# Decode delta rule of a hybrid decoder step: new values spread by transposes, or by a broadcast read of DRAM

## The chip, the cores and the metric

The kernel runs on one core of one Trainium2 chip. The metric is the device time of one execution in microseconds. The profile is of one further execution; its times count from the start of its span.

## The reference, cut to what matters

One layer of a decoder, for 256 prompt tokens and 8 decode tokens (one for each of 8 batch entries): a normed input times a wide matrix `w_in`, sparse attention on one side, a gated delta rule on the other, gates, and three output projections. The change lies in the delta rule of the decode tokens. For each of 8 entries and 8 heads there is a state S of 128x128, and one step is

```python
S = exp(g) * S
v_new = beta * (v - k @ S)
S = S + outer(k, v_new)
o = q @ S
```

The kernel gets k @ S and q @ S from the old state (both scaled by exp(g)) and adds (k . q) v_new to the second, so that o is known before S is updated. The updated S is an output, 1 MB for each pair of entries.

## The kernel before, in words

Nearly all work is projections in fp32 by three products of fp32r parts. Weights come in halves of 128 x 8 x 128 (512 KB, `raw`, issued on SP, three buffers); ScalarE copies the high part `hi` (L332), VectorE subtracts the low part `lo` (L333; three buffers each), and TensorE does 24 matmuls `acc` per half (L205), into one of two PSUM buffers. Two halves make a unit of 128 output columns; the units of the first output projection (letters `p` and `P`) are of one half. A unit ends with its evacuation: to a gate (`ev_gate`, L1504), an output gate (`ev_z`, L1489 to L1493), or, for `p`, a VectorE operation that folds PSUM into the gate tile (L1511). The order of the units is the string `ORDER`.

Everything else is written as generators that run between the matmuls: the main loop (L1627 to L1636) loads half i+4, splits half i+2, multiplies half i in two parts, and after each part calls `tick()`, which lets each active generator go on to its next `yield` (`yield n` rests n ticks). So the place of an instruction in the program is set by ticks. The framework's planner then orders each engine's queue when the kernel is built: VectorE, ScalarE and TensorE as its own timing suggests, an instruction emitted later moving ahead of one that it takes for not ready. SP and POOL keep the emitted order (L165). On the chip every queue is in order.

`g_gdn_dec` (L1364) is the delta rule of the decode tokens, `g_gdn` (L1128) that of the prompt; both start after the last `qkv` unit and run side by side. `g_gdn_dec` goes through the 8 entries in four pairs (`b0`, L1429). For a pair it multiplies the state `sst` by k and q (`sw`, 16 matmuls), brings the rows back (`swr`, `swt`), and gets the new values `dvn` (L1445), 16 columns of 128, and the output `dod` (L1446, L1447). Then the update: a new value lies along the partitions, and must be the same in all partitions and run along the columns. So TensorE transposes one column, broadcast to 128x128, into PSUM, 64 times in all, four to a group (`vnb`):

```python
for hh in range(4):
    c = (4 * hg + hh) * 8 + b0 + b
    tr(p4[:, 128 * hh:128 * hh + 128], vn[:, c:c + 1].to_broadcast([128, 128]))
yield 3
```

ScalarE scales the state (L1459) and VectorE adds PSUM times k (L1460). After the pair ScalarE's queue stores the state (`o_Ss`, L1463) and loads that of the next pair but one. A pair takes 36 ticks by its yields. When all are done, `odec` lets `g_gdn` put the decode output into `oB`, which the `Z` units need (L1485 waits for it by ticking).

Large tiles share one pool of `NS` slots of 8448 bytes per partition (`slot`, L169). A tile takes a slot when one is free and gives it back after its last use. `g_gdn` uses POOL's queue for the triangular inverse: `At` goes to DRAM and back (`ad`, `prod`, L1190 and L1197), its result too (`td`, `U`, `TI`, L1210 to L1216). The conv state of the decode tokens, `cd`, has a tile of its own.

Of the kernel before, what the change touches and what calls it, by code (L numbers as in the profile page):

```python
# [144 lines left out]
def program(tc, A):  # L145
# [8 lines left out]

    NS = 13
    cp = pool("cp")
# [12 lines left out]
    def slot(name, shape, dt=F32):  # L169
        return s8.tile(shape, dt, tag="s8", name=name)  # L170
# [70 lines left out]
    acc2 = cp.tile([128, 128], F32, name="acc2")  # L241
    cd = cp.tile([128, 24, 3, NB], F32, name="cd")
    cpo = cp.tile([128, 24, 3], F32, name="cpo")
# [5 lines left out]
    S.activation(warm, warm, AF.Exp)  # L249

    active, rest = [], {}

# [248 lines left out]
    def g_qstat(h):  # L501
# [7 lines left out]
        if h == 7:  # L509
# [16 lines left out]
            for g in range(2):  # L526
                V.scalar_tensor_tensor(o[:, g], qr[:, 4 * g:4 * g + 4, :], P("qw"),
                                       rd.rearrange("p (g r b) -> p g r b", g=2, r=4)[:, g], ALU.mult, ALU.mult)
            qx = slot("qm", [128, 640])
            G.memset(qx, 0.0)  # L530
            L["qdp"] = qdp = qx[:, 0:128]
# [520 lines left out]
    def ev_qkv(j):  # L1052
        def f(ps):
            k, h = j // 8, j % 8
            if h == 0:
                L["qkv", k] = slot("qkvr", [128, 8, TT])
                if k == 0:
                    SP.dma_start(cd, A["cst8"])
                if k == 1:
                    L["ktk"] = slot("ktk", [128, 2, 8, 128])  # L1060
                if k == 2:
                    L["vbt"] = slot("vbt", [128, 2, 8, 128])
            r = L["qkv", k]
            S.activation(r[:, h, :], ps[:, 0:TT], AF.Copy)
            V.tensor_copy(cpo[:, j, :], r[:, h, TP - 3:TP])
            if j == 23:
                G.dma_start(A["o_conv"], cpo)
            if h == 7:
                G.dma_start(A["o_convs"][:, 8 * k:8 * k + 8, 2, :], r[:, :, TP:TT])
            start(g_conv(j))  # L1070
        return f
# [292 lines left out]
    def g_gdn_dec():  # L1364
# [7 lines left out]
        state(0)  # L1372
        state(2)
        G.dma_start(A["o_convs"][:, :, 0:2, :], cd[:, :, 1:3, :])
        cw = P("cw").rearrange("p (j i) -> p j i", i=4)
# [11 lines left out]
        V.scalar_tensor_tensor(cv, th, 1.0, cv, ALU.add, ALU.mult)  # L1387
        sq = tp.tile([128, 16, NB], F32, name="dsq", tag="dsq", bufs=2)
        S.activation(sq, cv[:, 0:16], AF.Square)
        x = tp.tile([72, 2, 64], F32, name="dx", tag="dsq", bufs=2)  # L1390
        V.memset(x, 0.0)
# [10 lines left out]
        mm(pt[:, 128:256], ones[0:72, :], x.rearrange("p a c -> p (a c)"))  # L1402
        r = tp.tile([128, 128], F32, name="dr", tag="dsq", bufs=2)
        rsq(r, pt[:, 0:128], 1.0, 4 * EPS, [128, 128])
        eb = tp.tile([128, 2, 64], F32, name="deb", tag="deb")
        S.activation(eb, pt[:, 128:256].rearrange("p (a c) -> p a c", a=2), AF.Copy)
# [4 lines left out]
        q, k, v = f64(cv[:, 0:8]), f64(cv[:, 8:16]), f64(cv[:, 16:24])  # L1411
        wq = tp.tile([128, 80, 2], F32, name="wq", tag="wq")
        V.memset(wq[:, 64:80], 0.0)
# [10 lines left out]
        V.tensor_copy(kq, p2[:, 0:64])  # L1424
        od = tp.tile([128, 64], F32, name="dod", tag="dod")
        vn = tp.tile([128, 64], F32, name="dvn", tag="dvn")
        hb3 = lambda a: a.rearrange("p (h b) -> p h b", h=8)
        yield 2
        for b0 in range(0, NB, 2):  # L1429
# [14 lines left out]
            a3 = lambda t: t.rearrange("p (h b) -> p b h", h=8)[:, b0:b0 + 2]  # L1444
            V.tensor_sub(a3(vn), a3(u), pv[:, 0])  # L1445
            V.tensor_mul(a3(od), a3(vn), a3(kq))  # L1446
            V.tensor_add(a3(od), a3(od), pv[:, 1])  # L1447
            yield 4
            for b in range(2):
                for hg in range(2):  # L1450
                    p4 = PGD("vnb")
                    for hh in range(4):
                        c = (4 * hg + hh) * 8 + b0 + b
                        tr(p4[:, 128 * hh:128 * hh + 128], vn[:, c:c + 1].to_broadcast([128, 128]))
                    yield 3
                    for hh in range(4):
                        h = 4 * hg + hh
                        c = h * 8 + b0 + b
                        S.activation(ss[:, b, h, :], ss[:, b, h, :], AF.Copy, scale=eb[:, 0, c:c + 1])  # L1459
                        V.scalar_tensor_tensor(ss[:, b, h, :], p4[:, 128 * hh:128 * hh + 128], k[:, c:c + 1],  # L1460
                                               ss[:, b, h, :], ALU.mult, ALU.add)
                    yield 4
# [239 lines left out]
def build(m):  # L1702
    nc = _bacc.Bacc("TRN2", target_bir_lowering=False, num_devices=1, dynamic_dma_scratch_size=8192)
    A = {}
    for k, a in m.items():
        A[k] = nc.dram_tensor(k, a.shape, mybir.dt.from_np(a.dtype), kind="ExternalInput").ap()
    for k, s in OUTS.items():
        A[k] = nc.dram_tensor(k, s, F32, kind="ExternalOutput").ap()
    with tile.TileContext(nc, schedule_with_timeline_sim=True) as tc:
        program(tc, A)  # L1710
    nc.finalize()
    return nc
# [29 lines left out]
```

## Time and profile before

| | |
|---|---|
| median of 3 runs | 1135.54 us (1135.36 to 1137.25) |
| the profiled execution | 1137.88 us |
| its span | 1136.2 us |
| granted TensorE clock, mean | 0.994 |
| TensorE (PE) busy | 1112.4 us, 98% |
| VectorE (DVE) busy | 697.1 us, 61% |
| ScalarE (ACT) busy | 572.7 us, 50% |
| POOL busy | 144.2 us, 13% |

Busy time is the time in which an engine has an instruction at work; matmuls overlap, so the start-to-start distance says what one costs. A group of instructions is written as line, engine, operation, output<-inputs. "Idle before" or square brackets name the wait just before an instruction and what ended it.

### The profile page before, as it was taken

What the parts mean: (1) busy time and instruction counts of PE and PEld (TensorE: products, weight loads), DVE (VectorE), ACT (ScalarE), POOL (GpSimd) and SP (SyncE); (2) the same over time, 40 slices, a digit from 0 to 9 for tenths busy, and PEclk for the clock granted to TensorE, in tenths of its full rate; (3) what the DMA queues carried; (4) which work ended last, traced back from release to release, by engine and by line L of the source; (5) the groups of instructions that cost most, each with busy time, mean ns of one, the idle gap of its engine ahead of it and who ended that gap; (6) DMA issues with size and microseconds to landing.
All of it is one profiled execution on the core that took longest, in us unless ns stands there. A gap on an engine that the chain in (4) does not pass through costs nothing.

```text
span 1136.2 us, 25323 instructions
## 1 busy us (share of the span) xinstructions
PE 1112.4 (98%) x9558; PEld 1069.3 (94%) x9558; DVE 697.1 (61%) x1523; ACT 572.7 (50%) x1138; POOL 144.2 (13%) x227
## 2 busy tenths in 40 slices
PE   4999999999999999999999999999999999999998
PEld 3989999999999987897989999999999999999998
DVE  3578565443657776783566577677547575487443
ACT  4445655444634766673454465545344554444332
POOL 4430244200001310113022100102000000000000
PEclk9989999999999999999999899999999999999999
DMA  9873676435445784568998755657454355556663
GB/s 302 255 241 124 202 205 203 152 95 160 161 138 177 218 214 135 159 196 220 281 390 291 268 174 176 201 179 220 138 187 148 119 165 177 181 184 223 201 236 125
DMA packets 77069, 222.17 MB, mean 196 GB/s; under 512 B 10625, under 2 KB 27850, under 8 KB 75410
## 3 DMA queue, kind: packets, MB, share of 16 engines
q1 hardware_dynamic: 59346, 164.36, 44.7%
q0 software_dynamic: 15008, 44.98, 13.8%
q10 hardware_dynamic: 2592, 11.21, 2.6%
q8 instruction: 75, 1.23, 0.4%
q14 instruction: 48, 0.39, 0.1%
HBM read 202.90 MB, written 17.60 MB: 194 GB/s over the span
## 4 chain that ended last, share of the span: by engine, by line
PE 92%; DVE 1%; ACT 0%; issue 0%; ACTq 0%
PE acc L205 77%; PE inv L205 1%; PE po L205 1%; PE gtr L202 1%; PE pvo L205 1%; PE ps L205 1%; PE gsc L205 1%; PE cf L205 1%; PE kk L205 1%; PE vnb L202 1%; PE uw L205 1%; DVE xt L306 1%; PE pst L202 0%; PE og L205 0%; PE wsc L205 0%; PE kvtr L202 0%
## 5 line engine op out<-in xcount | busy, mean ns | idle before, releaser
L333 DVE TENSOR_TENSOR lo<-raw,hi 128x1024 fp32r<-128x1024 f32 (+1 forms) x250 | 304.8, 1220 | 212.5 <-ACT hi L332 206.1
L205 PE MATMUL acc<-xh,hi 128*128 128x264 f32 (+1 forms) x1488 | 433.8, 292 | 0.0
L332 ACT ACTIVATE hi<-raw 128x1024 fp32r<-128x1024 f32 (+1 forms) x250 | 263.9, 1056 | 329.7 <-PE acc L205 269.0
L205 PE MATMUL acc<-xl,hi 128*128 128x264 f32 (+1 forms) x1488 | 426.9, 287 | 0.5 <-issue 0.5
L205 PE MATMUL acc<-xh,lo 128*128 128x264 f32 (+1 forms) x1488 | 426.3, 287 | 0.0
L205 PEld LDWEIGHTS acc<-xh,hi 128*128 128x128 f32 (+1 forms) x1488 | 281.0, 189 | 7.6 <-issue 7.0
L205 PEld LDWEIGHTS acc<-xh,lo 128*128 128x128 f32 (+1 forms) x1488 | 280.0, 188 | 2.7 <-issue 2.2
L205 PEld LDWEIGHTS acc<-xl,hi 128*128 128x128 f32 (+1 forms) x1488 | 281.1, 189 | 1.5 <-issue 1.0
L205 PE MATMUL acc<-hi,w1h 128*128 128x254 f32 (+1 forms) x512 | 148.1, 290 | 15.9 <-ACT hi L409 15.9
L205 PE MATMUL acc<-lo,w1h 128*128 128x254 f32 (+1 forms) x512 | 147.4, 288 | 3.4 <-DVE lo L410 3.2
L205 PE MATMUL acc<-hi,w1l 128*128 128x254 f32 (+1 forms) x512 | 145.7, 285 | 0.0
L410 DVE TENSOR_TENSOR lo<-rawc,hi 128x512 fp32r<-128x512 f32 (+2 forms) x136 | 84.0, 656 | 52.5 <-ACT hi L409 48.1
L205 PEld LDWEIGHTS acc<-hi,w1h 128*128 128x128 f32 x512 | 98.4, 192 | 16.0 <-ACT hi L409 15.9
L409 ACT ACTIVATE hi<-rawc 128x512 fp32r<-128x512 f32 (+2 forms) x136 | 74.7, 599 | 62.7 <-PE acc L205 58.0
L205 PEld LDWEIGHTS acc<-lo,w1h 128*128 128x128 f32 x512 | 99.2, 194 | 4.8 <-DVE lo L410 4.5
L205 PEld LDWEIGHTS acc<-hi,w1l 128*128 128x128 f32 x512 | 99.0, 193 | 0.1
L386 POOL DMA_DIRECT2D rawc<-ccmp x125 | 67.3, 538 | 98.2 <-issue 72.3
L205 PE MATMUL acc<-oh,hi 128*128 128x264 f32 x256 | 73.5, 287 | 0.0
L205 PE MATMUL acc<-oh,lo 128*128 128x264 f32 x256 | 72.9, 285 | 0.0
L205 PE MATMUL acc<-ol,hi 128*128 128x264 f32 x256 | 72.7, 284 | 0.0
L205 PE MATMUL acc<-mh,hi 128*128 128x264 f32 x256 | 72.6, 284 | 0.0
L205 PE MATMUL acc<-ml,hi 128*128 128x264 f32 x256 | 72.5, 283 | 0.0
(452 smaller groups left out, 1476.4 us busy)
## 6 DMA issues: line engine op xcount, KB each, us to landing
raw<-win SPq DMA_DIRECT2D x184, 512.0 KB, 3.5
raw<-wpab SPq DMA_DIRECT2D x32, 512.0 KB, 3.9
raw<-wo SPq DMA_DIRECT2D x32, 512.0 KB, 4.3
rawc<-ccmp SPq DMA_DIRECT2D x126, 128.0 KB, 2.7
rawc<-ccmp POOLq DMA_DIRECT2D x125, 128.0 KB, 3.3
raw<-w SPq DMA_DIRECT2D x8, 512.0 KB, 7.6
wk<-winK SPq DMA_DIRECT2D x8, 512.0 KB, 11.1
o_wk<-wk POOLq DMA_DIRECT2D x8, 512.0 KB, 9.0
```

What stands on the lines that cost most here:

```text
L202: T.transpose(out, in_, ident[0:n, 0:n])
L205: T.matmul(out, lhsT, rhs, start=start, stop=stop, **k)
L306: V.scalar_tensor_tensor(xt[i][:, k, :], xt[i][:, k, :], P("nw")[:, kk:kk + 1], rx, ALU.mult, ALU.mult)
L332: S.activation(self.hi, self.raw, AF.Copy)
L333: V.tensor_sub(self.lo, self.raw, self.hi)
L386: e.dma_start(rawc[kv, b][j // 8][:, j % 8].rearrange("p s c g -> p (s c g)"), src[kv, bass.ds(r, 1)].rearrange("o d f -> (o d) f"))
L409: S.activation(h, src, AF.Copy)
L410: V.tensor_sub(l, src, h)
```

## The change

The group transposes go. Per pair, one transpose brings the 16 columns of the new values into 16 rows (`p4[0:16]`), VectorE copies them to SBUF (`vr`), POOL's queue writes them to DRAM (`vd`, 8 KB), and then reads them back broadcast to all 128 partitions into a slot `vw` (1 MB). The new values lie pair by pair in `vnp`, 16 columns side by side, for that. After 7 ticks come the 64 updates, which read `vw` in place of PSUM. `keep_in_program_order` (`late`) ties each of these to the VectorE instruction emitted before it, so that the planner can't move it ahead. A pair takes 29 ticks. `NS` is 14. Room for the slot comes from the conv state, which now lies in the slot of `qm`, from small tiles of the decode delta rule, which now lie in the two buffers `zz` of attention, and from half the scratch for POOL's DMA descriptors.

```diff
-    NS = 13
+    NS = 14
...
-    cd = cp.tile([128, 24, 3, NB], F32, name="cd")
...
+    late = tc.keep_in_program_order
...
-            qx = slot("qm", [128, 640])
-            G.memset(qx, 0.0)
+            qx = slot("qm", [128, 1216])
+            G.memset(qx[:, 0:640], 0.0)
+            L["cd"] = qx[:, 640:1216].rearrange("p (j i b) -> p j i b", j=24, i=3)
...
+        za, zb = (tp.tile([128, 384], F32, name=n, tag="zz", bufs=2) for n in ("dga", "dgb"))
+        cd = L.pop("cd")
...
-        sq = tp.tile([128, 16, NB], F32, name="dsq", tag="dsq", bufs=2)
+        sq = zb[:, 0:128].rearrange("p (h b) -> p h b", b=NB)
...
-        od = tp.tile([128, 64], F32, name="dod", tag="dod")
-        vn = tp.tile([128, 64], F32, name="dvn", tag="dvn")
+        od, vn = za[:, 288:352], zb[:, 256:320]
+        vd = dp.tile([4, 16, 128], F32, name="vd")
...
-            V.tensor_sub(a3(vn), a3(u), pv[:, 0])
-            V.tensor_mul(a3(od), a3(vn), a3(kq))
+            vnp = vn[:, 8 * b0:8 * b0 + 16]
+            vn3 = vnp.rearrange("p (b h) -> p b h", b=2)
+            V.tensor_sub(vn3, a3(u), pv[:, 0])
+            V.tensor_mul(a3(od), vn3, a3(kq))
             V.tensor_add(a3(od), a3(od), pv[:, 1])
-            yield 4
+            yield 2
+            p4 = PGD("vnt")
+            tr(p4[0:16, 0:128], vnp)
+            vr = tp.tile([16, 128], F32, name="vnr", tag="a", bufs=NA)
+            V.tensor_copy(vr, p4[0:16, 0:128])
+            vw = slot("vw", [128, 2, 8, 128])
+            G.dma_start(vd[b0 // 2], vr)
+            G.dma_start(vw.rearrange("p b h d -> p (b h d)"),
+                        vd[b0 // 2:b0 // 2 + 1].rearrange("o r d -> o (r d)").to_broadcast([128, 2048]))
+            yield 7
             for b in range(2):
                 for hg in range(2):
-                    p4 = PGD("vnb")
-                    for hh in range(4):
-                        c = (4 * hg + hh) * 8 + b0 + b
-                        tr(p4[:, 128 * hh:128 * hh + 128], vn[:, c:c + 1].to_broadcast([128, 128]))
-                    yield 3
                     for hh in range(4):
                         h = 4 * hg + hh
                         c = h * 8 + b0 + b
                         S.activation(ss[:, b, h, :], ss[:, b, h, :], AF.Copy, scale=eb[:, 0, c:c + 1])
-                        V.scalar_tensor_tensor(ss[:, b, h, :], p4[:, 128 * hh:128 * hh + 128], k[:, c:c + 1],
-                                               ss[:, b, h, :], ALU.mult, ALU.add)
+                        late(V.scalar_tensor_tensor(ss[:, b, h, :], vw[:, b, h, :], k[:, c:c + 1], ss[:, b, h, :],
+                                                    ALU.mult, ALU.add))
                     yield 4
...
-    nc = _bacc.Bacc("TRN2", target_bir_lowering=False, num_devices=1, dynamic_dma_scratch_size=8192)
+    nc = _bacc.Bacc("TRN2", target_bir_lowering=False, num_devices=1, dynamic_dma_scratch_size=4096)
```

## Rows read from the trace of the kernel before

**Rows 1.** The page's busy times, share of the span, instructions.

```profile
PE 1112.4 (98%) x9558; PEld 1069.3 (94%) x9558; DVE 697.1 (61%) x1523; ACT 572.7 (50%) x1138; POOL 144.2 (13%) x227
```

**Rows 2.** TensorE's waits, 100 us to the end: total, times, longest.

```profile
PE pvo L205 <- ACT wP L798: 0.6, 1, 0.6
PE acc L205 <- issue: 0.5, 1, 0.5
```

**Rows 3.** The chain that ended last, shares of the span by line.

```profile
by line: PE acc L205 76.6%; PE inv L205 1.4%; PE po L205 1.4%; PE gtr L202 1.2%; PE pvo L205 1.2%; PE ps L205 1.0%; PE gsc L205 0.9%; PE cf L205 0.7%; PE kk L205 0.6%; PE vnb L202 0.6%; PE uw L205 0.6%; DVE xt L306 0.5%; PE pst L202 0.5%; P
```

**Rows 4.** Windows: stretch, length, busy (x instructions) PE, PEld, DVE, ACT, POOL; PEclk, DMA, GB/s.

```profile
640.00:930.00 290.00, 290.00 (x2731) 284.73 (x2731) 190.18 (x440) 143.64 (x301) 13.43 (x24) 1.00 0.52 168
...
65.00:70.00 5.00, 5.00 (x43) 4.83 (x41) 4.15 (x4) 4.80 (x8) 1.61 (x3) 1.00 0.76 210
70.00:75.00 5.00, 2.44 (x12) 2.41 (x12) 5.00 (x9) 1.27 (x3) 1.61 (x3) 0.70 0.78 228
75.00:80.00 5.00, 5.00 (x28) 4.79 (x28) 2.15 (x7) 1.15 (x2) 1.62 (x3) 0.62 0.97 338
...
635.00:640.00 5.00, 5.00 (x25) 5.00 (x26) 1.90 (x7) 1.49 (x3) 0.00 (x0) 0.52 1.03 367
640.00:645.00 5.00, 5.00 (x36) 5.00 (x36) 0.00 (x0) 0.30 (x2) 0.00 (x0) 0.80 0.45 148
```

**Rows 5.** Timeline of TensorE around one group: start, duration, instruction.

```profile
732.14 0.28 PE L205 MATMUL acc<-xh,lo 128*128 128x264 f32 x1
732.26 0.60 PE L202 MATMUL vnb<-cst,dvn 128*128 128x128 f32 x4
732.62 0.37 PE L205 MATMUL acc<-xh,hi 128*128 128x264 f32 x1
732.83 0.28 PE L205 MATMUL acc<-xl,hi 128*128 128x264 f32 x1
732.94 0.28 PE L205 MATMUL acc<-xh,lo 128*128 128x264 f32 x1
```

**Rows 6.** The tile `vnb`: ns min/median/max, first and last start.

```profile
L202 PE MATMUL vnb<-cst,dvn x64: 270/272/323, 672.1 to 874.5; 128*128 128x128 f32 x64
L1460 DVE SCALAR_TENSOR_TENSOR sst<-vnb,dcv,sst x64: 339/344/353, 672.7 to 875.7; 128x128 f32<-128x128 f32 x64
```

**Rows 7.** Timeline of POOL from 600 us, and one VectorE row.

```profile
724.22 4.49 POOL L1190 DMA_DIRECT2D ad<-At  x8 [94.01 <-DVE At L1180]
757.44 0.57 POOL L1197 DMA_DIRECT2D prod<-ad  x1 [28.74 <-DVE zt L1491]
...
724.49 1.22 DVE L333 TENSOR_TENSOR lo<-raw,hi 128x1024 fp32r<-128x1024 f32 x1
```

**Rows 8.** The tile `raw`, 640 to 930 us: splits, and loads to landing.

```profile
L332 ACT ACTIVATE hi<-raw x77: 1040/1060/1071, 645.0 to 926.5; 128x1024 fp32r<-128x1024 f32 x77
...
DMA to landing us min/median/max: 3.2/3.4/4.0
```

**Rows 9.** Landing rows of two tiles: the states `sst`, then `td`.

```profile
DMA to landing us min/median/max: 6.7/9.2/11.7
...
DMA to landing us min/median/max: 2.0/3.9/5.7
```

**Rows 10.** ScalarE's waits, 640 to 930 us: total, times, longest.

```profile
ACT hi L332 <- PE acc L205: 77.3, 45, 3.8
...
ACT hi L332 <- DMA raw<-win: 3.3, 2, 2.2
```

**Rows 11.** The tiles `gate` and `At`: ns min/median/max, first and last start.

```profile
L1511 DVE SCALAR_TENSOR_TENSOR gate<-gate,acc x16: 414/429/430, 769.0 to 861.2; 128x264 f32<-128x264 f32 x16
...
L205 PE MATMUL inv<-U,At x96: 217/275/323, 804.5 to 854.5; 128*128 128x64 f32 x64, 64*64 64x64 f32 x32
```

**Rows 12.** Timeline of ScalarE's queue, 834 to 840 us.

```profile
834.12 0.35 ACTq L1463 DMA_DIRECT2D o_Ss<-sst  x1
...
839.05 0.35 ACTq L1370 DMA_DIRECT2D sst<-stS  x1
```

**Rows 13.** Timeline of TensorE: the wait near 70 us.

```profile
72.59 0.58 PE L205 MATMUL acc<-lo,w1h 128*128 128x254 f32 x1 [2.56 <-DVE lo L410]
```

More of the change, by code (lines that the diff above doesn't have):

```diff
@@ L1057, in f @@
                 if k == 0:
-                    SP.dma_start(cd, A["cst8"])
+                    SP.dma_start(L["cd"], A["cst8"])
                 if k == 1:
@@ L1387, in g_gdn_dec @@
         V.scalar_tensor_tensor(cv, th, 1.0, cv, ALU.add, ALU.mult)
-        sq = tp.tile([128, 16, NB], F32, name="dsq", tag="dsq", bufs=2)
+        sq = zb[:, 0:128].rearrange("p (h b) -> p h b", b=NB)
         S.activation(sq, cv[:, 0:16], AF.Square)
-        x = tp.tile([72, 2, 64], F32, name="dx", tag="dsq", bufs=2)
+        x = zb[0:72, 128:256].rearrange("p (a c) -> p a c", a=2)
         V.memset(x, 0.0)
@@ L1402, in g_gdn_dec @@
         mm(pt[:, 128:256], ones[0:72, :], x.rearrange("p a c -> p (a c)"))
-        r = tp.tile([128, 128], F32, name="dr", tag="dsq", bufs=2)
+        r = zb[:, 0:128]
         rsq(r, pt[:, 0:128], 1.0, 4 * EPS, [128, 128])
-        eb = tp.tile([128, 2, 64], F32, name="deb", tag="deb")
+        eb = za[:, 0:128].rearrange("p (a c) -> p a c", a=2)
         S.activation(eb, pt[:, 128:256].rearrange("p (a c) -> p a c", a=2), AF.Copy)
@@ L1411, in g_gdn_dec @@
         q, k, v = f64(cv[:, 0:8]), f64(cv[:, 8:16]), f64(cv[:, 16:24])
-        wq = tp.tile([128, 80, 2], F32, name="wq", tag="wq")
+        wq = za[:, 128:288].rearrange("p (c w) -> p c w", w=2)
         V.memset(wq[:, 64:80], 0.0)
```

## Prediction

> **What bounds the kernel now.** I read the engines' busy times first: TensorE has work in 98% of the span and weight loads in 94%, VectorE in 61%, ScalarE in 50%, POOL in 13% [rows 1]. Next, TensorE's waits after the start: from 100 us to the end it waited 1.1 us in all, in two waits [rows 2]. So whatever leaves TensorE's stream shortens the kernel, as long as no other engine makes it wait; whatever leaves another engine is worth nothing. The chain that ended last, by line, says the same: matmuls nearly throughout, with 0.6% in `vnb`, the 64 broadcast transposes that the change takes out [rows 3]. Then the stage itself, 640 to 930 us: TensorE busy in all of its 290.00 us, the granted clock 1.00 in the mean (2.4 GHz), the DMA engines at 0.52 [rows 4].
>
> **What goes, on the path.** Four transposes make a group, and there are 16 groups (4 pairs of batch entries, 2 entries, 2 halves of the heads). In the timeline of TensorE, one group stands between two projection matmuls: the last `acc` before it starts at 732.14, the second one behind it at 732.83 [rows 5]. Neighbouring `acc` start 0.12 us apart (732.83 to 732.94), so without the group these 0.69 us would be 0.24: a group costs 0.45 us, and 16 cost 7.2. The chain's 0.6% of 1136.2 us is 6.2 to 7.4, if it is rounded from 0.55 to 0.65. I take 7.2, because the timeline shows the change between the two kinds of matmul too.
>
> **What comes onto the path.** One transpose of 128x16 per pair, four in all. Inside a group a transpose takes 0.36 / 4 = 0.09 us, and the change of kind behind it another 0.09 (732.62 to 732.83 against 0.12); 0.2 us each, 0.8 in all. Net 7.2 - 0.8 = 6.4 us; with the chain's ends 5.4 to 6.6.
>
> **What comes beside it.** Four copies of 16x128 on VectorE, fewer columns than an update's 128x128 and so at most its 0.34 us each [rows 6]: 1.4 in all. The 64 updates stay, and read SBUF in place of PSUM; no row has this operation from SBUF, and I leave them at 0.34. This lies on an engine with 39% to spare. POOL gets eight DMAs of about 0.57 us [rows 7]; it issues none between 640 and 724 us. Shared tiles for the small arrays, the conv state inside the `qm` slot and the halved descriptor scratch cost nothing that I can price: the two `zz` buffers have been idle since attention, and no row shows what the scratch is worth. Were POOL's early page loads held up by the smaller one, the price would be that of the stall at 70 us, 5.4 us (rival 1); a gain is excluded, since less scratch frees no issue. I take 0, since those loads are the same 128 KB pieces as before.
>
> **The broadcast read: is it in time?** The update waits for a chain that the trace lacks; I bound it by rows. Transpose 0.27 us [rows 6], copy 0.2 (estimate, under 0.34), perhaps one split ahead of it on VectorE 1.22 [rows 8], issue 0.56, landing of a small DRAM write 2.0 to 5.7 [rows 9], issue 0.57, landing of 1 MB. For this last the nearest rows are the state loads, as large and with the same 8 KB per partition: 6.7, 9.2, 11.7 us (shortest, median, longest) [rows 9]. Shortest 0.27 + 0.2 + 0.56 + 2.0 + 0.57 + 6.7 = 10.3 us; middle, with the split and 9.2, 14.0; longest, with the split, 5.7 and 11.7, 20.2. I take the middle.
> Against it: the generator lets 7 ticks pass. There are 77 splits from 645.0 to 926.5 [rows 8], so 3.7 us to a half and 1.85 to a tick: 13.0 us. VectorE would then stand about 1 us at the first update. Behind it in its queue is the next `lo`, for which TensorE waits. But `hi` and `lo` have three buffers: when TensorE ends a half, the next split may start, and it has two halves, 7.4 us, until it needs it; the split takes 1.06 + 1.22. That leaves 5.1 us, so a wait at the update reaches TensorE only when the chain exceeds 13.0 + 5.1 = 18.1 us. ScalarE's rows show this reserve: its splits waited 77.3 us for TensorE, and 3.3 us for their data [rows 10]. The cover is gone in the stretch of single-half `p` units, where VectorE must empty PSUM once per half: there the reserve is 3.7 - 0.43 = 3.3 us [rows 11]. I take 0 us; the bounds are 0 (nothing on TensorE waits here today, so nothing can be gained) and the price of rival 1.
>
> **Slots.** By the code 13 large tiles are alive around 680 us (two parts of `qkv`, `ktk`, `vbt`, two gates, `oA`, two states, `At`, `aT`, `oh`, `ol`), that is all of them. The trace shows it: POOL stood 28.74 us before `prod`, until the last `zt` had read `oA`, and the last state was loaded at 839.05, 4.9 us behind the store at 834.12 [rows 7, 12]. The first `vw` gets slot 14. The next gate tile must wait for that `vw` or the first state; the second `vw` finds room when the keys are released near 724. The third will probably find none until `At` is last read at 854.5 [rows 11], and POOL stands there. Queued behind it are only the last pair's two DMAs and the store of the prompt state, since `td` and the `U` loads are emitted before. What moves back is the update and store of the last two states, which nothing but their slots and the output waits for (`odec` needs `od`, not the update), and some 200 us of projection follow. Cost 0; gain 0.
>
> **Sum.** The profiled execution took 1137.88 us around its span of 1136.2; less 6.4 it is 1131.5. The median of the runs is 2.3 us below it, so I predict **1129 us**. A measurement can tell about 0.2%, 2.3 us, from no change.
>
> **Rival 1: the pinned updates meet a late broadcast** (slower). Place: VectorE at the first update of a pair, in emitted order, with `lo` behind it. It decides from 18.1 us on, or 16.3 where `p` units run; the long chain of 20.2 gives a TensorE wait of 2 to 4 us. What such a wait costs is shown at 70 us: TensorE waited 2.56 us [rows 13], and in the 10 us from 70 to 80 did 12 and 28 matmuls in its two windows, where the window before holds 43, the granted clock being down to 0.62 [rows 4]. 46 matmuls at 0.116 us are 5.4 us. Two pairs cost 10.8 and give 1140, four 1151. For it: the read shares the 16 DMA engines with the weight loads. Against it: those land in 3.2 to 4.0 us throughout the stage [rows 8], though state loads and stores of the same size ran among them.
> Were each of a pair's two POOL issues held until a VectorE operation of 1.2 us ends, the middle chain would be 16.4 us, a hair over the reserve in the `p` stretch. The trace speaks against it: eight DMAs issued from 724.22 took 4.49 us, 0.56 each, while VectorE ran a 1.22 us split at 724.49 [rows 7]. For a hold at another place I leave 0.02 of the chance. The Trainium skill, SBUF — State Buffer, section "SBUF: two separate sides", gives that hold as a rule: VectorE operations that take the shared port pair shut GpSimd out, so that a DMA issued there waits for its descriptors. By that rule the hold would be usual; these eight issues do not show it. In all **0.21**.
>
> **Rival 2: given back elsewhere** (no change). Slots and ticks alter what the planner puts next to what, over the whole kernel. From 635 us on the clock was at 0.52 of full, so near 1.2 GHz, behind a run of short matmuls and with TensorE busy all the time; the two windows from 635 to 645 hold 25 and 36 matmuls where 43 are the full rate [rows 4]: 25 x 0.116 = 2.9 us. Two more such stretches (5.8) or one stall (5.4) leave a gain of 0.6 to 1.0 us: about 1135. For it: both losses exist now. Against: the change adds no run of short matmuls. **0.14**. That the change doesn't do what it says I count here: the transposes are plainly gone from the code.
>
> **Rival 3: more than the transposes** (faster). The fourteenth slot could free the start: POOL's loads there and the split order decide the 5.4 us at 70 us. With that gone, 1123.7; with the slow stretch gone as well, 1120.8. For it: TensorE has no other loss. Against: the wait at 70 us is for `lo`, an operation of VectorE [rows 13], whose order a slot need not change. **0.10**.
>
> **How the numbers follow.** The forecast, 6.4 us less, with one slow stretch of 2.9 us lost or gained by another order (1126 to 1132): **0.55**, because every wait that could undo it has a reserve in the rows. Faster: forecast and rival 3, 0.65. Within 0.2%: rival 2, 0.14. Slower: rival 1, 0.21. The range 1123 to 1140 leaves out the far half of rival 3 (0.05) and those cases of rival 1 with three stalls or more (some 0.10).
>
> **What would show it.** `vnb` gone and four new transposes: TensorE has 60 fewer matmuls and weight loads. TensorE busy without a gap from 640 to 930 us, at 1.00. Broadcast landing near 9 us. VectorE's waits for `vw` small, and none by TensorE for `lo`. Wrong would be: TensorE waits above 2 us after 100 us, clock below 0.9 in a stage where it was 1.00, or a `vw` landing above 12 us.

## The result, and the profile after

The change makes the kernel slower: the median is 1145.36 us (1142.16 to 1150.29, six runs) against 1137.04 of the kernel before in the same runs, a ratio of 1.0084 (95%: 1.0069 to 1.0099). The profiled execution took 1142.16 us, the lowest of the six, around a span of 1140.5, and that of the kernel before, 1137.88, lies above its median, so what the two show of the loss is rather too little.

The page's busy times and the chain by engine, to hold against [rows 1]:

```profile
PE 1107.4 (97%) x9498; PEld 1062.7 (93%) x9498; DVE 698.8 (61%) x1527; ACT 574.2 (50%) x1138; POOL 149.0 (13%) x235
...
PE 78%; issue 11%; DMA 4%; DVE 3%; SPq 1%; POOLq 1%; POOL 1%; ACT 0%; ACTq 0%
```

TensorE has 60 instructions and 5.0 us of work less, as forecast, and yet the span is 4.3 us longer. Its waits in the whole span tell of stalls that the kernel before did not have after 100 us [rows 2] (13.8 us of the first line, one wait, is the start; 1.3 us of it lies after 100 us):

```profile
PE acc L205 <- ACT hi L409: 16.7, 3, 13.8
PE uw L205 <- ACT wT L1299: 5.5, 2, 3.4
...
PE acc L205 <- issue: 1.9, 2, 1.0
PE sw L205 <- DMA sst<-stS: 0.7, 1, 0.7
```

Windows say where. The columns are those of [rows 4]. Before:

```profile
130.00:140.00 10.00, 10.00 (x80) 9.95 (x79) 5.37 (x16) 6.25 (x20) 4.10 (x9) 1.00 0.86 284
525.00:545.00 20.00, 19.49 (x222) 16.88 (x224) 8.71 (x19) 8.54 (x15) 5.93 (x6) 1.00 0.95 223
...
860.00:880.00 20.00, 20.00 (x174) 19.76 (x174) 18.11 (x64) 6.63 (x11) 0.00 (x0) 1.00 0.47 163
880.00:900.00 20.00, 20.00 (x174) 20.00 (x172) 11.08 (x24) 11.89 (x36) 0.00 (x0) 1.00 0.38 128
```

After:

```profile
130.00:140.00 10.00, 8.52 (x63) 8.06 (x63) 4.98 (x15) 6.14 (x18) 3.91 (x8) 1.00 0.50 158
525.00:545.00 20.00, 18.13 (x188) 15.24 (x186) 6.66 (x16) 7.18 (x13) 5.99 (x6) 0.91 0.83 195
...
860.00:880.00 20.00, 16.33 (x137) 15.72 (x135) 18.68 (x62) 5.97 (x8) 0.56 (x1) 1.00 0.65 242
880.00:900.00 20.00, 18.21 (x144) 18.21 (x145) 11.89 (x35) 8.42 (x26) 0.00 (x0) 0.91 0.37 128
```

Two of the places lie long before the delta rule. At 130 us ScalarE's queue holds a split of `w1h` (whose tile is a slot of the big pool) ahead of the page splits `hi`, and stands for its load; at 527 to 534 six indirect gathers come in one bunch, where the kernel before has them as four and two. TensorE stands behind each; in the first place it waits for a page split, in the second the profile shows nothing that it waits for (`issue`), so that the gathers are its cause is not shown. First ScalarE and TensorE near 132 us, then POOL and TensorE near 530, of the kernel after:

```profile
131.96 1.06 ACT L367 ACTIVATE w1h<-raw 128x1024 fp32r<-128x1024 f32 x1 [1.65 <-DMA raw<-w]
...
133.48 0.40 PE L205 MATMUL acc<-hi,w1h 128*128 128x286 f32 x1 [1.28 <-ACT hi L409]
...
526.96 0.98 POOL L892 DMA_INDIRECT gv<-cslv,idx  x1 [9.62 <-issue]
...
533.33 1.14 POOL L892 DMA_INDIRECT gv<-cslv,idx  x1 [0.30 <-issue]
...
533.96 0.28 PE L205 MATMUL acc<-xh,lo 128*128 128x264 f32 x1 [0.86 <-issue]
...
535.38 0.28 PE L205 MATMUL acc<-xl,hi 128*128 128x264 f32 x1 [1.01 <-issue]
```

The third place is the prompt's `uw` stage. POOL's broadcast reads of the third and fourth pair:

```profile
854.26 0.59 POOL L1460 DMA_DIRECT2D vw<-vd  x1 [58.09 <-PE inv L205]
...
863.66 0.56 POOL L1460 DMA_DIRECT2D vw<-vd  x1 [8.31 <-PE inv L205]
```

VectorE's timeline of the kernel after there, then TensorE's:

```profile
862.90 4.29 DVE L1469 SCALAR_TENSOR_TENSOR sst<-vw,dcv,sst 128x128 f32<-128x128 f32 x16 [0.85 <-DMA vw<-vd]
...
869.88 4.28 DVE L1469 SCALAR_TENSOR_TENSOR sst<-vw,dcv,sst 128x128 f32<-128x128 f32 x16
...
874.19 0.41 DVE L1298 COPY vbt<-uw 128x256 f32<-128x256 f32 x1
...
876.29 0.49 PE L205 MATMUL uw<-vbt,U 128*128 128x128 f32 x2 [2.01 <-ACT wT L1299]
...
881.79 0.79 PE L205 MATMUL uw<-vbt,U 128*128 128x128 f32 x2 [3.45 <-ACT wT L1299]
```

The third read goes out when `At` has been read, at 854.26 as forecast (854.5), and the fourth 9.4 us later. So 32 updates fall into two blocks of 16 in the one stage where TensorE waits for VectorE's copies out of PSUM (`vbt`, then ScalarE's `wT`). VectorE's busy time from 860 to 880 is nearly that of before (18.68 against 18.11): its order is what differs. Before, the last pair's updates came in fours there, two of them:

```profile
870.67 1.12 DVE L1460 SCALAR_TENSOR_TENSOR sst<-vnb,dcv,sst 128x128 f32<-128x128 f32 x4
...
872.82 1.12 DVE L1460 SCALAR_TENSOR_TENSOR sst<-vnb,dcv,sst 128x128 f32<-128x128 f32 x4
```

To see what each place costs in the end, I took the starts of the same ScalarE evacuation in two traces. The table holds the start in the kernel named, less the start before, in us; from the last row to the end of the span the shift hardly moves (+4.3 at the end of the kernel after). Each column is one execution. Some lie away from their medians: those of "after", "slots, held" and "no updates, held" were the fastest of their runs, that of "after, held" the slowest. The columns behind the second are experiments below.

| start before (operation) | after | slots alone | slots, held | late updates skipped | after, held | no updates, held |
|---|---|---|---|---|---|---|
| 98.0 (`cy`) | -1.6 | -2.3 | -1.2 | -1.4 | -1.2 | -1.7 |
| 147.5 (`cy`) | +0.3 | +1.5 | -1.2 | +2.9 | -1.2 | -1.7 |
| 540.1 (`qkvr`) | +3.4 | +4.7 | -1.8 | +6.1 | -1.9 | -1.9 |
| 644.7 (`zt`) | +1.8 | +4.7 | -3.4 | +6.2 | +3.3 | -3.4 |
| 857.6 (`gate`) | -0.6 | +6.4 | -1.6 | +3.0 | +3.7 | -6.5 |
| 953.9 (`gate`) | +4.6 | +6.4 | -1.6 | +0.7 | +9.5 | -8.7 |

The kernel after loses about 5 us by 540 and 5.2 from 857.6 to 953.9, and gains some 4 between.

### The profile page after: what moved, and what is told of

It is laid out like the page before. It is cut to its first block, busy times and chain, and to the rows that moved or that the text cites. A ratio compares the mean times of both kernels' runs of the same rounds, so it can differ in the third digit from the quotient of the medians.

```text
span 1140.5 us, 25217 instructions
## 1 busy us (share of the span) xinstructions
PE 1107.4 (97%) x9498; PEld 1062.7 (93%) x9498; DVE 698.8 (61%) x1527; ACT 574.2 (50%) x1138; POOL 149.0 (13%) x235
## 4 chain that ended last, share of the span: by engine, by line
PE 78%; issue 11%; DMA 4%; DVE 3%; SPq 1%; POOLq 1%; POOL 1%; ACT 0%; ACTq 0%
PE acc L205 65%; PE po L205 1%; PE pvo L205 1%; PE gtr L202 1%; DMA raw<-w 1%; DVE lo L333 1%; PE ps L205 1%; DMA rawc<-ccmp 1%; PE gsc L205 1%; DVE sst L1469 1%; POOLq L385 1%; DMA vw<-vd 1%; DMA U<-td 1%; SPq L385 1%; SPq L386 1%
```

## Experiments: the parts of the change

My theory after these readings: two independent losses, the fourteenth slot (it alters the order of the program long before its first use by `vw`) and the late block of updates. Rivals: the pins, or the block alone.

**Slots alone.** The memory edits and `NS = 14` of the change, with the transposes and updates of before:

```diff
-            vw = slot("vw", [128, 2, 8, 128])
...
+                    p4 = PGD("vnb")
...
-                        late(V.scalar_tensor_tensor(ss[:, b, h, :], vw[:, b, h, :], ...
+                        V.scalar_tensor_tensor(ss[:, b, h, :], p4[:, 128 * hh:128 * hh + 128], ...
```

> The kernel before with the fourteenth slot and all the memory edits (conv state in the qm slot, zz buffers, scratch of 4096), but with the 64 transposes and PSUM updates kept. Theory A (two separate losses): the loss of about 4 us before 637 us comes with the slot, through the earlier gathers, and the loss of 6 us from 876 us on comes with the late updates. Then this kernel shows the first alone: about 1141 us (1139 to 1143), the first gate evacuation about 4 us later than before (632.8), no TensorE wait at the uw stage. Theory B (all of the loss belongs to the broadcast and its updates): 1136 to 1138 us. If the early loss is only chance of one profiled execution: 1136 to 1138 us too, and the first gate evacuation near 633.

1144.68 us against 1136.25, 1.0069 (1.0048 to 1.0091). Most of the loss is there without one broadcast read. Its windows at the two early places are as bad as those of the change:

```profile
130.00:140.00 10.00, 8.20 (x51) 7.79 (x50) 3.86 (x13) 4.80 (x13) 4.27 (x8) 0.83 0.48 155
525.00:545.00 20.00, 18.27 (x156) 14.79 (x156) 5.36 (x14) 6.51 (x12) 5.98 (x6) 0.91 0.79 178
```

**A tile of its own for `vw`, 13 slots.**

```diff
-    NS = 14
+    NS = 13
...
-            vw = slot("vw", [128, 2, 8, 128])
+            vw = tp.tile([128, 2, 8, 128], F32, name="vw", tag="vw")
```

> The kernel after with vw in a tile of its own outside the slot pool, and 13 slots again: the third and fourth broadcast no longer wait for At. Theory A: the 32 updates of the last two pairs leave the uw stage, TensorE's waits on wT there (5.5 us) vanish, the early loss goes too since the slots are as before, and the gain of the transposes stays: 1130 to 1133 us. Theory B (late broadcasts or pinned updates themselves cost the time): still 1137 us or more. Theory A without its part on the slots before 637 us: about 1135.

1137.16 us, 1.0010 (0.9996 to 1.0024): level with before, not below it. The expected 1130 to 1133 us were missed. The early stalls and the late block are gone, but the updates of the first pairs now stand in a VectorE queue that has no idle time from 690 to 703 us. TensorE, then ScalarE:

```profile
701.83 0.40 PE L202 MATMUL rrow<-cst,dec 128*128 128x128 f32 x2 [2.16 <-DVE aT L1183]
...
706.45 0.59 PE L205 MATMUL acc<-xh,hi 128*128 128x264 f32 x1 [1.29 <-ACT gate L1513]
...
706.00 0.67 ACT L1513 ACTIVATE gate<-acc 128x264 f32<-128x264 f32 x2 [2.06 <-DMA o_Ss<-sst]
```

The last row is the gate that stands until a state's slot is stored; from 705 to 710 the granted clock was 0.50 (1.2 GHz).

**No pins.** The change with `late(...)` taken off the updates.

```diff
-                        late(V.scalar_tensor_tensor(ss[:, b, h, :], vw[:, b, h, :], ...))
+                        V.scalar_tensor_tensor(ss[:, b, h, :], vw[:, b, h, :], ...)
```

> The kernel after without the program-order ties on the 64 updates. Theory A: the updates of the last two pairs still become ready only after 854 us, in the same blocks of 16, so the TensorE waits at the uw stage stay: 1142 to 1147 us, as after. Theory B in its form that the pins hold lo and the PSUM copies behind the updates: 4 to 6 us faster than after, 1136 to 1140 us.

1145.17 us, 1.0081 (1.0062 to 1.0100), the change's own loss. The pins are not its cause.

**Late updates skipped.** The change without the 32 updates of the third and fourth pair, whose states are then only scaled.

```diff
+                        if b0 < 4:
                             late(V.scalar_tensor_tensor(...))
+                        elif b == hg == hh == 0:
+                            late(V.tensor_copy(eg8[0:4], vw[0:4, b, h, 0:8]))
```

> The kernel after without the 32 updates of the last two pairs (each pair's broadcast is still read, one small copy keeps its wait; the two stored states are left scaled only). Theory A: without the two blocks of 16 updates VectorE reaches the PSUM copies in time, the TensorE waits on wT at 876 and 881 us (5.5 us) and the slow clock behind them vanish: 5.5 to 7.5 us less than after, 1136 to 1140 us. Rival C (it is the transfers: two 1 MB broadcasts and two 1 MB stores among the weight loads that hold TensorE up there): 1142 to 1147 us, and the waits on wT stay or turn into waits on hi and raw.

1136.77 us, 1.0001 (0.9988 to 1.0014): 8.6 us below the change. Its windows are whole there, and the table shows 2.3 us gained between 857.6 and 953.9 where the change loses 5.2:

```profile
860.00:880.00 20.00, 20.00 (x174) 19.59 (x173) 16.40 (x54) 7.40 (x12) 0.00 (x0) 1.00 0.36 125
880.00:900.00 20.00, 20.00 (x173) 20.00 (x172) 9.18 (x14) 11.86 (x35) 0.00 (x0) 1.00 0.37 122
```

So both parts of the theory stand: the slot costs by itself, and so does the block where it lies. What the same updates cost at another place is a question of its own, taken up below.

## Experiments: the slot kept back until it is needed

A tile takes the fourteenth slot at the start and gives it back where the delta rule begins:

```diff
+    L["hold"] = slot("hold", [128, 2112])
+    V.memset(L["hold"][:, 0:1], 0.0)
...
+        V.memset(L.pop("hold")[:, 1:2], 0.0)
```

Three of the next four runs were meant to do this and did not: with nothing to wait for, the second memset ran at 1.4 us in the trace, so that the slot was free nearly from the start. They are read as further kernels with fourteen slots, in other orders. The fourth has no hold.

**Slots alone, with this hold:**

> The first experiment (slots and memory edits, transposes kept) with one slot held empty from the start of the program until the decode delta rule begins near 630 us: 13 slots are usable before, 14 after; the scratch of 4096 and the moved tiles stay. Theory A2 (the early loss is the fourteenth slot's: page loads and gathers run ahead in bunches): the losses at 130 us and at 533 us go, 5 to 7 us less than without the hold, 1138 to 1140 us. Rival D (the halved descriptor scratch or the moved tiles cost the time): 1143 to 1146 us.

1139.39 us, 1.0033 (1.0019 to 1.0046). TensorE was busy for 7.93 us of 130 to 140, so that stall is there, but for all 20.00 of 525 to 545.

**The change, with this hold:**

> The kernel after with the same held slot. Theory A2: the early loss goes and the late block of updates stays, with its TensorE waits for wT at the uw stage: 1138 to 1141 us. Rival D: 1143 to 1147 us, as after. If the early loss is part of the spread between executions: 1143 to 1147 us too, with the losses at 130 and 533 us in place.

1140.79 us, 1.0047 (1.0031 to 1.0063); 7.78 and 20.00 us in those windows. That this result and the one above lie in the ranges expected of a slot that is kept back is luck: it was not kept back.

**The same, and the updates of pairs three and four put off** until the decode output stands in `oB` (the writes of `vd` stay where they were):

```diff
+            if b0 < 4:
+                yield from update(b0, ss)
+            else:
+                held[b0] = ss
...
+        yield from wait("oB")
+        for b0 in (4, 6):
+            yield from update(b0, held.pop(b0), 28 if b0 == 4 else 7)
```

> The kernel after with the held slot, and with the broadcast read and the 32 updates of the last two pairs put behind oB (from some 930 us on, four updates in four ticks), where VectorE is 40 to 60 per cent busy; odec is marked before them. Theory A2: neither loss is left, the gain of the transposes shows: 1130 to 1134 us. If updates read from SBUF cost TensorE time wherever they run: 1137 us or more, with TensorE waits between 930 and 1000 us.

1141.20 us, 1.0045 (1.0024 to 1.0066). The block is gone (TensorE busy in all 40 us from 860 to 900), but a wait at the last state's `sw` is new, 3.1 us, and the busy time of 790 to 800 is 6.89 us; in the first pair TensorE stood 1.4 us for `zt` and 1.3 for `edl`.

**Put off, without a hold:**

> The kernel after with the deferred updates of the third and fourth pair, without the held slot. Theory A2: the waits for wT at the uw stage go, the early loss stays: 1136 to 1140 us, 5 to 7 us above the same kernel with the hold and near the kernel that left these updates out (1136.8). If the late updates only move their cost: 1142 us or more.

1141.78 us (1135.5 to 1147.7), 1.0052 (1.0034 to 1.0070): the same picture, with 3.5 us at `sw`.

Then a hold that holds: its second use reads a result that is there only when the delta rule begins, and ran near 622 us in the traces (620.8 to 624.3).

```diff
-        V.memset(L.pop("hold")[:, 1:2], 0.0)
+        V.tensor_copy(L.pop("hold")[:, 0:24], cpo[:, :, 0])
```

**The memory edits with 13 slots** (slots alone, `NS = 13`):

> The kernel before with all the memory edits (scratch of 4096, conv state in the qm slot, zz buffers) and the transposes kept, but with 13 slots. Theory A3 (the early loss is the fourteenth slot's alone: with it the planner puts two splits w1h of the next weights ahead of page splits on ScalarE, where they wait for their load near 131 us, and the value gathers bunch near 530 us): the same as before, 1135 to 1138 us, no TensorE wait for hi near 131 us. Rival D (scratch or moved tiles): 1139 us or more.

1136.61 us against 1135.97, 1.0004 (0.9990 to 1.0017). The conv state, the shared small tiles and the halved scratch cost nothing.

**Slots alone, held until 622 us:**

> The slots-alone kernel with a hold that does hold: the earlier hold was released at once, since its second use depended on nothing and the planner moved it to the start; here the second use copies the conv outputs that are only there near 630 us. So 13 slots are usable until 630 us and 14 after, transposes kept. Theory A3: the ScalarE order near 131 us is that of before again, and the losses there and at 533 us go: 1135.5 to 1138.5 us. If the fourteenth slot costs time after 630 us too: 1139 to 1141 us.

1137.44 us, 1.0021 (1.0007 to 1.0035), against 1.0069 without the hold; from the 1.0004 of thirteen slots it can't be told apart. Its two windows are whole:

```profile
130.00:140.00 10.00, 10.00 (x79) 9.95 (x79) 5.85 (x18) 7.30 (x22) 4.29 (x8) 1.00 0.87 272
525.00:545.00 20.00, 20.00 (x249) 17.93 (x248) 9.77 (x21) 8.96 (x16) 5.93 (x6) 1.00 0.95 227
```

The first window is whole in every kernel with thirteen slots until 622 us (TensorE busy in all 10.00 us), where each of the eight with fourteen from the start has 7.27 to 9.04. The start of the same `cy` evacuations says it in time: between 98.0 and 147.5 us the eight lose 1.3 to 4.6 us against the kernel before, and the eleven others -0.1 to +0.2. The bunch of gathers is in all eight too, but only four of them stalled behind it (18.13 to 18.27 us busy, and 1.7 to 3.2 us lost between 147.5 and 540.1); the other four were busy for 20.00 and lost nothing there. What decides that stays open.

**The change, held until 622 us:**

> The kernel after with the hold that holds until 630 us. Theory A3: the early loss of 4 to 7 us goes, the block of late updates with its waits for wT stays: 1138 to 1141 us. Rival: if only the late block matters, 1143 to 1147 us.

1140.31 us, 1.0045 (1.0031 to 1.0059). By the ratios the early slot is worth 0.39% of the change's 0.84%, some 4.4 us, but this is a difference of two medians whose intervals are 0.15% to either side, and the change with the first hold, which had fourteen slots from the start and its stall at 130 us, stood at 1.0047. So the size of the early part in the change is not settled. The late block is still there: 5.5 us of waits for `wT`. (The profiled execution, 1147.28, was this kernel's slowest; its +5.2 between 540.1 and 644.7 in the table has nothing to do with the block.)

## Experiments: what is left, and other places for the updates

**No updates at all.** The change, held, without the 64 updates, so that the states are only scaled; the reads, the stores, the slot and the 29 ticks stay:

```diff
-                        late(V.scalar_tensor_tensor(...))
+                        if b == hg == hh == 0:
+                            late(V.tensor_copy(eg8[0:4], vw[0:4, b, h, 0:8]))
```

> The kernel after with the late-released hold and without all 64 updates (the states are stored scaled only; broadcasts are read, one small copy per pair keeps their wait). Theory V (what the early loss leaves over is VectorE: updates in the stages where it is full, rrow and kk near 700 us and uw near 875 us): no TensorE wait in either stage, the gain of the transposes shows, 1129 to 1132 us. Theory X (slots, 29 ticks a pair, and 1 MB transfers cost it): 1136 us or more, as 1140.3 with the updates.

1132.95 us against 1136.88, 0.9968 (0.9955 to 0.9980), the only run below the kernel before. From 644.7 on it gains 5.3 us (table); the forecast for the transposes was 6.4, and 5.4 by the chain's lower end. That execution, 1129.11, was the fastest of ten; by the medians the gain is 0.36% (4.1 us) against the memory edits with 13 slots and 0.53% (6.0 us) against slots alone, held, both with the transposes. So the reads and the short pairs cost nothing that shows as long as the updates are away. TensorE is whole where it was not:

```profile
680.00:710.00 30.00, 30.00 (x276) 29.66 (x275) 17.53 (x39) 18.16 (x42) 0.00 (x0) 1.00 0.59 212
...
860.00:880.00 20.00, 20.00 (x173) 20.00 (x172) 13.39 (x43) 8.20 (x15) 0.00 (x0) 1.00 0.37 119
```

The three ratios make a sum: -0.32% without updates, +0.77% for the 64 updates on VectorE, +0.39% for the early slot, 0.84% together. The 32 late updates alone made 0.83% in the change (1.0084 against 1.0001), as much as all 64 here, so in the order of the change the medians leave no cost for the first 32.

**Pairs three and four put off, pairs as long as before.** The deferred edit with the good hold, 14 ticks ahead of the updates of pairs one and two (`update(b0, ss, 14)`), and 14 ticks (`yield 14`) behind pairs three and four:

> The kernel after with the hold that holds, the deferred updates of the last two pairs, and pairs as long as before: seven more ticks before the updates of the first two pairs and fourteen between the third and fourth, so that TensorE does not come to the third state before it has landed (3.1 us of wait and slow clock behind it in the earlier deferred kernel). Theory A3 with this third loss: nothing is left but the gain, 1129 to 1133 us. If 1136 us or more, the updates that read SBUF cost TensorE time in the first two pairs as well, and the trace from 675 to 760 us has to show it.

1141.22 us, 1.0036 (1.0024 to 1.0049). No wait for a state and none in `uw`, but three in the first pairs, where TensorE stood 2.1 us for VectorE's `aT`, 2.1 for `edl` and 1.2 for `aT` again. The updates stand seven ticks later than in the change here, and so the first two pairs cost after all.

**Put off, pairs one and two as in the change** (lead 7, and `yield 17` behind pairs three and four):

> The kernel after with the late-released hold, the first two pairs as in after (29 ticks, on VectorE), and the updates of the last two pairs put behind oB and spread, with seventeen ticks between the third and fourth pair so that the fourth state has landed. It differs from the held kernel (1140.3) in the place of the last 32 updates alone. Theory V, the block at the uw stage being the largest part: 1133 to 1136 us, no wait for wT. If the first two pairs cost the rest: 1137 us or more, with the waits between 675 and 800 us.

1140.11 us (1134.9 to 1143.4), 1.0027 (1.0012 to 1.0042). The waits of TensorE:

```profile
PE sw L205 <- DMA sst<-stS: 4.8, 1, 4.8
...
PE acc L205 <- DVE zt L1516: 1.4, 1, 1.4
PE kk L205 <- DVE edl L1169: 1.0, 1, 1.0
```

VectorE and TensorE in its timeline at the two places:

```profile
687.13 1.14 DVE L1446 SCALAR_TENSOR_TENSOR sst<-vw,dcv,sst 128x128 f32<-128x128 f32 x4 [3.42 <-DMA vw<-vd]
...
798.76 1.93 PE L205 MATMUL sw<-sst,dga 128*32 128x128 f32 x32 [4.83 <-DMA sst<-stS]
```

And the window around the second:

```profile
790.00:800.00 10.00, 5.17 (x57) 4.99 (x59) 2.45 (x2) 3.10 (x5) 2.76 (x5) 0.81 1.03 271
```

The first of these rows is the late broadcast of rival 1, followed within 5 us by the two small waits of TensorE, for `edl` and `zt`. The second, and the window, are another thing: the last state is loaded at 787.2, beside the `U` loads of the inverse, with the DMA engines full (1.03), and lands after 13.7 us; the granted clock is 0.81 there, between its levels of 1.2 and 2.4 GHz. Before, the load went out at 839.05 [rows 12]. With slots alone, in pairs of 36 ticks, it goes out at 776.00, beside the `U` loads too, but its `sw` comes at 854 us; with 29 ticks `sw` comes at 799. The change has 0.7 us of this wait.

**Updates on GpSimd.** If VectorE has no room, another engine might. Held, with each update group as a product and a sum of 128x512:

```diff
+                    G.tensor_tensor(w4, w4, k4.to_broadcast([128, 4, 128]), ALU.mult)
+                    G.tensor_tensor(s4, s4, w4, ALU.add)
```

> The kernel after with the late-released hold and the updates on GpSimd, four heads at a time, as a product and a sum of 128x512 each (32 of either), since vw and the state are both in SBUF. Theory V: near the kernel without updates, 1130 to 1134 us. If GpSimd and VectorE hinder each other at SBUF, or the updates on POOL's queue hold back the inverse's DMAs: 1138 us or more, with longer VectorE operations or later ad, td and U.

1154.10 us, 1.0142 (1.0118 to 1.0166). GpSimd's work now stands in the queue that issues the inverse's loads. The second pair's last group comes behind those loads, so its tiles keep their slots, and the loads wait for another one:

```profile
836.67 0.58 POOL L1214 DMA_DIRECT2D U<-td  x1 [59.67 <-DVE gate L1523]
...
845.66 1.06 POOL L1472 TENSOR_TENSOR vw<-vw,dcv 128x512 f32<-128x512 f32 x1
```

**The same with `vw` in its own tile and 13 slots:**

> The second experiment (vw in a tile of its own, 13 slots) with the updates on GpSimd in the same way. Theory V: without updates on VectorE the stall at 700 us (aT, then the gate's slot behind the state's store) is shorter, 1131 to 1135 us against 1137.2. If the gate's slot decides there, which waits for the state's update and store: 1137 us or more.

1154.96 us, 1.0156 (1.0133 to 1.0179): those loads again, after a wait of 59.3 us.

**A pair's groups issued together, so that none is left behind in the queue** (the ticks of a pair change with it):

```diff
+            for b in range(2):
+                for hg in range(2):
...
+                    G.tensor_tensor(s4, s4, w4, ALU.add)
+            yield 8
```

> As the GpSimd kernel with the hold, but with the updates of a pair issued together, so that those of the first two pairs stand ahead of ad on POOL's queue and those of the last two behind the U loads; there the second pair's last group stood behind 60 us of waiting, held its vw slot and so kept the U loads from starting until 836 us, and the inverse came late. Theory V: with the inverse on time again, 1130 to 1135 us. If GpSimd's 2 us operations among a full VectorE at 680 to 700 us cost TensorE time: 1137 us or more, with waits there.

1144.54 us, 1.0065 (1.0046 to 1.0083). The loads are in time (from 774 us). What is left is `wT`, late again (7.5 us of waits), and VectorE's operations take longer beside GpSimd's: a `lo` 2.07 us, against 1.22 [rows 7]. Two rows of POOL and one of VectorE:

```profile
733.45 1.24 POOL L1476 TENSOR_TENSOR vw<-vw,dcv 128x512 f32<-128x512 f32 x1
734.76 2.15 POOL L1477 TENSOR_TENSOR sst<-sst,vw 128x512 f32<-128x512 f32 x1
...
733.70 2.07 DVE L333 TENSOR_TENSOR lo<-raw,hi 128x1024 fp32r<-128x1024 f32 x1
```

**Only pairs three and four on GpSimd** (`if b0 >= 4` around the same two lines):

> The kernel after with the late-released hold and only the updates of the last two pairs on GpSimd; the first two pairs stay on VectorE, pinned. Nothing but the prompt state's store is queued behind them on POOL. Theory V, with the block at the uw stage as the largest part: the waits for wT go, 1133 to 1136 us against 1140.3 with that block on VectorE. If the block was not the cause: 1139 us or more.

1141.93 us, 1.0052 (1.0035 to 1.0069). In the `uw` stage VectorE's four scalings took 0.93 us each beside GpSimd's operations (POOL's row stands first), and TensorE waited for `wT` as long as ever (6.3 us in two waits):

```profile
862.39 2.28 POOL L1477 TENSOR_TENSOR sst<-sst,vw 128x512 f32<-128x512 f32 x1
...
863.45 3.74 DVE L1291 TENSOR_SCALAR ktk<-ktk,kds 128x128 f32<-128x128 f32 x4
...
878.78 0.80 PE L205 MATMUL uw<-vbt,U 128*128 128x128 f32 x2 [4.97 <-ACT wT L1299]
```

The same four in the run with the late updates skipped:

```profile
869.15 0.86 DVE L1291 TENSOR_SCALAR ktk<-ktk,kds 128x128 f32<-128x128 f32 x4
```

No version that reads the broadcast and does the whole computation came out below the kernel before; the one with `vw` in its own tile and 13 slots equals it. Every version that gave the updates another place missed its expectation on the slow side: other losses took the place of the block's.

## Why the prediction was wrong

**Right.** TensorE has 60 instructions less, and the transposes are worth 5.3 us from the delta rule on, 4.1 to 6.0 by medians (forecast 6.4, ends 5.4 to 6.6: about the lower end). The new transpose takes 0.27 us and the copy 0.28 (forecast 0.27, and under 0.34), an update from SBUF 345 ns (0.34). The broadcast is in time as far as TensorE is concerned. In the first pair:

```profile
678.95 0.58 POOL L1460 DMA_DIRECT2D vw<-vd  x1 [3.64 <-DMA vd<-vnr]
...
685.98 1.14 DVE L1469 SCALAR_TENSOR_TENSOR sst<-vw,dcv,sst 128x128 f32<-128x128 f32 x4 [1.60 <-DMA vw<-vd]
```

From the transpose at 673.9 to the landing at 686.0 it took 12.1 us (middle of the forecast 14.0), 7.0 of them for the read (forecast 9.2), and VectorE stood 1.60 us (forecast about 1); in the third pair it stood 0.85. The hold for which rival 1 left 0.02 was not seen: POOL's `vd` and `vw` issues took 0.50 to 0.59 us. But only five of these eight fell beside a VectorE operation, all of them splits, updates or operations on PSUM; beside a copy or a scaling from SBUF to SBUF none fell, and the rows of the forecast had a split alone, so for those the hold is neither shown nor excluded. The memory edits cost 0 (13 slots: 1.0004). The third `vw` waits until 854.26.

**Wrong, first: "What moves back is the update and store of the last two states, which nothing but their slots and the output waits for ... Cost 0."** When the work moves was forecast to the microsecond; that it is free was wrong. I asked who waits for the moved work, and named 200 us of projection as its cover. I did not ask what the moved work stands in front of. VectorE's queue at 862 to 874 us belongs to the `uw` stage, where it must empty PSUM between short products, and 16 updates in one piece are 4.3 us. The cost by the table is 7.5 us (5.2 lost where the kernel without those updates gains 2.3), and 8.6 by the medians. The text priced exactly such a cover gone for the `p` units, and left out this stage.

**Wrong, second: the fourteenth slot before 622 us was not a term of the sum.** It appears only in rival 3, as a gain. The whole program is ordered with the pool in it: a free slot lets `w1h` splits move ahead, and an in-order queue then stands for their load. Cost 0.39 to 0.48% (by the change and by slots alone, with and without the hold), 4 to 5 us, with the reserve made above for the change; the traces show 1.3 to 4.6 us lost at 130 us in all eight kernels with fourteen slots, and 1.7 to 3.2 near 533 us in four. For slots alone the slot is shown as the cause (1.0069 with fourteen, 1.0004 with thirteen, the code otherwise the same). That it acts by this split is read from the traces; no run moved the split alone.

**Wrong, third: a pair of 29 ticks has a price.** The free slot brings the last state's load forward, in the change to 787 us and into the inverse's loads, and the shorter pair brings TensorE to that state near 800 us, before it has landed. The change shows 0.7 us of wait for it, and the deferred kernels with such pairs 3.1 to 4.8. Without the pins, or without the updates, the load went out at 757 and 751 us, and there is no wait: the ticks cost only where the load goes out so late.

**The rivals.** Rival 1's mechanism is real, but small: where VectorE stood longest for `vw` (3.42 us, in the last deferred kernel), TensorE's waits behind it were 1.0 and 1.4 us; the stall that decided is another one of VectorE, for another reason. Rival 2 was right in kind, given back elsewhere by what the slots and ticks put next to what, and priced it at 5.4 to 5.8 us where it was some 13 (0.77% and 0.39%). Rival 3 had the slot's sign wrong. Measured is 1145.36; the range ended at 1140, because cases were priced one by one, and no case took the slot's and the block's losses together. Some 1.5 us of the miss lie in the base, a median of three runs (1135.54), where the six have 1137.04.

**Open.** Why four of eight kernels stalled at 533 us and four did not (three of the four that did were run on one chip, all that did not on another, so the chip is not excluded); how much of the change's own loss is the early slot's; and the shift of -3.4 to +1.0 us that traces have already at 98 us, where the programs hardly differ.

## What to carry to other kernels

Of work that is moved, ask two things: who waits for it, and what it lands in front of in its own in-order queue. A later place costs nothing only if the engine has no due work for the bound engine there. A resource added for one stage (a buffer in a shared pool) is free to all earlier stages as well, and here the planner used it there; add it with a dependency that keeps it back, and look at the trace from the first microsecond. To find such losses, compare the starts of the same instruction in two traces: the shift steps where time goes.

## What was not expected of the hardware

VectorE beside GpSimd: `ktk` scalings of 128x128 took 0.93 us instead of 0.22 (0.86 for four) beside GpSimd's 128x512 operations, and a `lo` 2.07 instead of 1.22; GpSimd's own sum took 2.28 beside a `lo` and those, and 1.26 to 1.35 otherwise in that run. The Trainium skill, SBUF — State Buffer, section "Who interferes with whom", says that the shared ports are an exclusive lock, and one of the two then waits; these rows agree: the `lo` of 733.70 began beside a product of GpSimd's and ended 1.08 us behind it, about its time alone, and the sum begun beside the rest of that `lo` took 2.15. I had tried GpSimd as free room, and in this stage it is not.

Small stalls have a tail: after TensorE's two waits of 2.01 and 3.45 us for `wT` the window from 880 to 900 has a granted clock of 0.91, between 1.2 and 2.4 GHz, and 144 matmuls against 174 before, with TensorE idle for 1.79 us of it.
